# Decayed GLA keys turned on VectorE and placed through DRAM, where TensorE transposed them per pair

## The chip, the cores and the metric

The kernel runs on one core of one Trainium2 chip. The metric is the device time of one execution in microseconds (us), taken as the median of several runs. TensorE (PE) multiplies matrices and loads its weights (PEld), VectorE (DVE) and ScalarE (ACT) work elementwise on SBUF and PSUM, GpSimd (POOL) here mostly issues stores, and SyncE (SP) issues loads.

## What is computed

The reference is one layer of a hybrid trunk: a shared input projection, then gated linear attention (GLA), multi-scale pooling and cross-attention, gated, summed and projected. What the change touches is the GLA recurrence of the prompt (4 heads, 1024 tokens, key dimension 128, value dimension 256, blocks of 64 tokens):

```python
b = jnp.cumsum(ab, axis=3)
b_last = b[:, :, :, -1:]
q_dec = qb * jnp.exp(b)
k_inv = kb * jnp.exp(-b)
k_end = kb * jnp.exp(b_last - b)
att = jnp.where(mask, jnp.einsum('bhncd,bhnsd->bhncs', q_dec, k_inv), 0.0)
o_intra = jnp.einsum('bhncs,bhnse->bhnce', att, vb)
dS = jnp.einsum('bhncd,bhnce->bhnde', k_end, vb)
...
o_inter = jnp.einsum('bhncd,bhnde->bhnce', q_dec, S_before)
```

`k_end`, the decayed keys, is what is turned. It comes with the key dimension on the partitions and the tokens along the free axis. `dS` sums over tokens, so TensorE wants it with the tokens on the partitions.

## The kernel before

The prompt's GLA runs in 16 chunks: 4 heads with 4 chunks of 256 tokens, and each chunk in two pairs (even and odd) of 128 tokens. It fills the span from about 392 to 740 us, at some 21.6 us per chunk, and is interleaved on PE with the large products of the input projection (called px in the rows: groups of three matmuls, lines 242 to 244) and with the steps of the sample tokens and the cross-attention. PE and SP work in the order in which the program issues. DVE, ACT and POOL work in an order that a scheduler sets when the program is built.

For each chunk there are these functions:

- `gla_load` (L896) has SP load the log decays (alc) and the keys and queries (kq).
- `gla_gates` (L903) makes the decays (bz), and from them the decayed queries and both forms of the keys. The last row, L935, leaves k_end in kq.
- `gla_within` (L938), once per pair, computes the scores within a block in two matmuls of 64 columns each (L944, L945), transposes 128 columns of k_end on PE into the other half of the same PSUM tile (L946), masks the scores on DVE (L947), and splits the whole tile of 256 columns into a high part (ACT, L223) and a low part (DVE, L224), both in one tile called ak.
- `gla_recur` (L952), once per pair, multiplies by the values: `mm3` (L242 to L244) does a product from the high and low parts in three matmuls, once with the turned keys (into td) and once with the scores (into to). L963 adds the old state's part. Then the state is advanced (st, L968), and the output copied and squared on ACT (L976, L977).
- `gla_values`, `gla_split` load and split the values (v, vsh). `gla_out` turns the output in 32 x 32 blocks on DVE (L992) and stores it with four stores on POOL (L994).

`gla_steps` sets the order of these per chunk n: gates of n+1, split of n, the even pair's `gla_within`, the recurrence of the odd pair of chunk n-1, the odd pair's `gla_within`, the loads for later chunks, the recurrence of the even pair, and the output of chunk n-1. `R(...)` takes the next tile from a ring of 14 buffers that most of these steps share, so that a tile's first writer waits for the last reader of the tile that had that place before.

Of the kernel before, what the change touches and what calls it, by code (L numbers as in the profile page):

```python
# [9 lines left out]
F32 = mybir.dt.float32  # L10
F32R = mybir.dt.float32r
# [7 lines left out]
P = 128  # L19
# [5 lines left out]
NH = 4  # L25
# [22 lines left out]
def trunk_kernel(ctx: ExitStack, tc: tile.TileContext,  # L48
# [159 lines left out]
    al_scr = scratch(2, "als", (P, HT))  # L208
    q_scr, k_scr = (scratch(2, s, PAIR) for s in ("qsc", "ksc"))
    vt_scr = scratch(NH, "vtsc", (T, DV))  # L210
    u_scr, xq_raw = (scratch(4, s, PAIR) for s in ("usc", "xqsc"))
    mix_scr = [None if n == 0 else scratch(4, f"mixsc{n}_", (P, 2, T)) for n in range(3)]
    on_scr = scratch(NH, "onsc", (DV // 32, 32, 2, 4, 2, 64))
# [690 lines left out]
    def gla_gates(h, c):  # L904
# [29 lines left out]
        act(z, z, AF.Exp, scale=1.0 / TAU)  # L934
        nc.vector.tensor_tensor(k, k, z, op=ALU.mult)  # L935
        gla["g", h, c] = kq, kiqi, decp

    def gla_within(h, pr):  # L938

        c, cs = pr // 2, slice((pr % 2) * P, (pr % 2 + 1) * P)  # L940
        kq, kiqi, _ = gla["g", h, c]
        kt, qd, ki, qi = (x[:, cs] for x in (kq[:, 0], kq[:, 1], kiqi[:, 0], kiqi[:, 1]))
        t = PZ()
        nc.tensor.matmul(t[0:64, 0:P], lhsT=ki[:, 0:64], rhs=qi, start=True, stop=True)  # L944
        nc.tensor.matmul(t[64:P, 0:P], lhsT=ki[:, 64:P], rhs=qd, start=True, stop=True)  # L945
        nc.tensor.transpose(t[:, P:2 * P], kt, ident)  # L946
        nc.vector.copy_predicated(t[:, 0:P], nmask, zeros)  # L947
        ak = R([2, DV], F32R, name="ak")
        split(ak[:, 0], ak[:, 1], t[:, :DV])
        gla["w", h, pr] = ak[:, 0], ak[:, 1]  # L950

    def gla_recur(h, pr):  # L952
        c, cs = pr // 2, slice((pr % 2) * P, (pr % 2 + 1) * P)
        hi, lo = gla["w", h, pr]
        vh, vl = (x[:, pr % 2] for x in gla["vs", h, c])
        _, kiqi, decp = gla["g", h, c]
        st = gla.get(("st", h))
        t = PZ()
        td, to = t[:, :DV], t[:, DV:]
        mm3(td, hi[:, P:], lo[:, P:], vh, vl, True, True)  # L960
        mm3(to, hi[:, :P], lo[:, :P], vh, vl, True, st is None)
        if st is not None:
            nc.tensor.matmul(to, lhsT=kiqi[:, 1, cs], rhs=st, start=False, stop=True)  # L963
        s2 = wk.tile([P, DV], F32, tag="st", name="st", bufs=2)
        if st is None:
            nc.vector.tensor_copy(s2, td)
        else:
            nc.vector.scalar_tensor_tensor(s2, st, decp[:, pr % 2:pr % 2 + 1], td, op0=ALU.mult, op1=ALU.add)  # L968
        gla["st", h] = s2
        if pr == 7:  # L970
            nc.gpsimd.dma_start(out=o_gla_p[h], in_=s2)
        if pr % 2 == 0:
            sq = wk.tile([P, 2], F32, tag="sq", name="sq", bufs=3)
            gla["o", h, c] = R([2, DV], name="on"), sq
        on, sq = gla["o", h, c]
        nc.scalar.activation(on[:, pr % 2], to, AF.Copy)  # L976
        nc.scalar.activation(to, to, AF.Square, accum_out=sq[:, pr % 2:pr % 2 + 1])  # L977
        if pr % 2:
            r = rstd_of(sq, 1.0 / DV)
            for j in range(2):  # L980
                nc.scalar.activation(on[:, j], on[:, j], AF.Copy, scale=r[:, j:j + 1])
# [87 lines left out]
    def gla_steps():  # L1069
# [7 lines left out]
        for n in range(N + 1):  # L1077
# [5 lines left out]
            if n < N:  # L1083
                gla_split(h, c)
                gla_within(h, 2 * c)
                yield 2
            if n > 0:
                gla_recur(ph, 2 * pc + 1)
                yield 2
                yield next(samples, 0)  # L1090
            if n < N:
                gla_within(h, 2 * c + 1)
                yield 2
                yield next(samples, 0)
# [471 lines left out]
```

## Time and profile before

| | us |
|---|---|
| median of 3 runs | 1442.61 (1440.45 to 1442.92) |
| the profiled execution: its own time | 1445.01 |
| the profiled execution: its span | 1443.3 |
| PE busy | 1417.4 |
| DVE busy | 916.2 |
| ACT busy | 679.0 |
| POOL busy | 222.1 |

The page of the profile covers one execution. A row such as `396.34 0.75 DVE L224 ... x2` gives the start in us from the start of the span, the length, the engine, the line, the operation, out<-in with the tiles' names, the shape, and the count of instructions put together; a bracket at its end gives the idle time before it and what ended it. Rows of the chain of waits give start, length, engine, tile and line. The PE rows of the timeline overlap, since matmuls are pipelined; their steady distance is 0.12 us. The granted clock is 1.00 through the whole GLA stage.

### The profile page before, as it was taken

To read this page: it belongs to the slowest core of one execution; us is meant where nothing else is said; L and a number is where in the kernel's file an instruction comes from. 1 tells how busy PE (TensorE), PEld (TensorE's weight loads), DVE (VectorE), ACT (ScalarE), POOL (GpSimd) and SP (SyncE) were. 2 spreads that over 40 slices of the span, in tenths; PEclk is the share of its full clock that TensorE was granted. 3 is DMA by queue.
4 is the path that set the end of the run, shared out by engine and by line. 5 is a ranking of instruction groups with operands and counts; after the bars stand their busy time and mean duration, and the time that the engine had idled before them with its cause. 6 is when DMAs were issued, how large, how long until landed. Compare 5 with 4: busy or idle time off the path is not lost.

```text
span 1443.3 us, 28179 instructions
## 1 busy us (share of the span) xinstructions
PE 1417.4 (98%) x10689; PEld 1356.1 (94%) x10689; DVE 916.2 (63%) x2123; ACT 679.0 (47%) x1575; POOL 222.1 (15%) x401
## 2 busy tenths in 40 slices
PE   8999999999999999999999999999999999999998
PEld 6899999989899999999999999999999999999876
DVE  6954756666687777767766778785672434554436
ACT  6743544443465666656654445444472432233212
POOL 3211111124342121212221111111010000000000
PEclk9999999999999999999999999999999999999999
DMA  9355665656656363554654455454694777632633
GB/s 329 125 165 169 217 218 187 207 175 165 198 155 193 115 192 129 182 176 126 187 167 150 149 188 170 159 184 163 204 298 134 234 257 249 234 104 79 224 118 116
DMA packets 183507, 259.42 MB, mean 180 GB/s; under 512 B 22204, under 2 KB 132564, under 8 KB 183364
## 3 DMA queue, kind: packets, MB, share of 16 engines
q1 hardware_dynamic: 159900, 183.87, 41.5%
q0 software_dynamic: 23328, 73.56, 14.7%
q8 instruction: 84, 1.38, 0.4%
q14 instruction: 51, 0.42, 0.1%
q10 hardware_dynamic: 144, 0.20, 0.0%
HBM read 180.47 MB, written 77.56 MB: 179 GB/s over the span
## 4 chain that ended last, share of the span: by engine, by line
PE 88%; DMA 5%; DVE 5%; issue 1%; ACT 1%; SPq 0%; POOL 0%; DVEq 0%; ACTq 0%; POOLq 0%
PE px L242 25%; PE px L243 25%; PE px L244 25%; DMA qb<-xqs 3%; PE pz L244 2%; PE pz L243 2%; PE pz L242 2%; DMA raw<-in_w_in_dram 1%; DVE kc L777 1%; PE pz L963 1%; PE pz L404 1%; PE pz L944 1%; PE pz L817 1%; PE pz L946 1%; PE pz L907 0%
## 5 line engine op out<-in xcount | busy, mean ns | idle before, releaser
L244 PE MATMUL px<-bh,wbl 128*128 128x384 f32 (+1 forms) x576 | 184.1, 320 | 0.0
L243 PE MATMUL px<-bl,wbh 128*128 128x384 f32 (+1 forms) x576 | 184.1, 320 | 0.0
L242 PE MATMUL px<-bh,wbh 128*128 128x384 f32 (+1 forms) x576 | 183.7, 319 | 0.0
L554 ACT ACTIVATE r<-px 128x258 f32<-128x258 f32 x240 | 89.9, 375 | 47.4 <-PE px L244 46.9
L242 PEld LDWEIGHTS px<-bh,wbh 128*128 128x128 f32 x576 | 108.3, 188 | 0.0
L243 PEld LDWEIGHTS px<-bl,wbh 128*128 128x128 f32 x576 | 108.2, 188 | 0.0
L244 PEld LDWEIGHTS px<-bh,wbl 128*128 128x128 f32 x576 | 108.2, 188 | 0.0
L242 PE MATMUL px<-ot,s1h 128*128 128x258 f32 x320 | 94.1, 294 | 0.0
L242 PE MATMUL px<-o,a12h 128*128 128x258 f32 x320 | 93.4, 292 | 0.0
L242 PE MATMUL px<-ot,s3h 128*128 128x258 f32 x320 | 93.2, 291 | 0.0
L242 PE MATMUL px<-o,s4h 128*128 128x258 f32 x320 | 93.0, 291 | 0.2 <-DVE c L636 0.2
L242 PE MATMUL px<-o,a11h 128*128 128x258 f32 x320 | 92.8, 290 | 0.0
L242 PE MATMUL px<-ot,a22h 128*128 128x258 f32 x320 | 92.6, 289 | 0.0
L242 PE MATMUL px<-ot,s2h 128*128 128x258 f32 x320 | 92.2, 288 | 0.0
L243 PE MATMUL px<-o,a11h 128*128 128x258 f32 x320 | 91.1, 285 | 0.3 <-DVE o L224 0.3
L243 PE MATMUL px<-o,a12h 128*128 128x258 f32 x320 | 91.1, 285 | 0.0
L244 PE MATMUL px<-o,a12l 128*128 128x258 f32 x320 | 91.0, 284 | 0.0
L244 PE MATMUL px<-ot,s1l 128*128 128x258 f32 x320 | 90.9, 284 | 0.0
L243 PE MATMUL px<-ot,s1h 128*128 128x258 f32 x320 | 90.8, 284 | 0.0
L244 PE MATMUL px<-o,a11l 128*128 128x258 f32 x320 | 90.6, 283 | 0.0
L243 PE MATMUL px<-ot,s2h 128*128 128x258 f32 x320 | 90.1, 281 | 0.5 <-DVE ot L224 0.5
L243 PE MATMUL px<-ot,a22h 128*128 128x258 f32 x320 | 90.5, 283 | 0.0
(471 smaller groups left out, 4634.3 us busy)
## 6 DMA issues: line engine op xcount, KB each, us to landing
raw<-in_w_in_dram SPq DMA_DIRECT2D x80, 512.0 KB, 4.0
msc<-c POOLq DMA_DIRECT2D x24, 516.0 KB, 4.8
brsc<-c POOLq DMA_DIRECT2D x24, 516.0 KB, 3.7
sig<-msc SPq DMA_DIRECT2D x24, 516.0 KB, 6.0
brr<-brsc SPq DMA_DIRECT2D x48, 256.0 KB, 5.2
wbr<-in_w_branch_dram SPq DMA_DIRECT2D x24, 512.0 KB, 5.5
acc<-sig POOLq DMA_DIRECT2D x16, 516.0 KB, 5.2
acc<-acc SPq DMA_DIRECT2D x16, 516.0 KB, 7.0
```

Source lines behind the costliest of these rows:

```text
L242: nc.tensor.matmul(out, lhsT=lh, rhs=rh, start=start, stop=False, skip_group_check=more)
L243: nc.tensor.matmul(out, lhsT=lh, rhs=rl, start=False, stop=False, skip_group_check=more)
L244: nc.tensor.matmul(out, lhsT=ll, rhs=rh, start=False, stop=stop, skip_group_check=more)
L404: nc.tensor.matmul(t[:, :DV], lhsT=memT[k // 2][:, k % 2, a * P:(a + 1) * P], rhs=raw[k // 2][:, k % 2], start=k == 0, stop=k == NK - 1)
L554: nc.scalar.activation(r, acc[c][:, :QT], AF.Copy)
L777: nc.vector.tensor_tensor_reduce(kc[:, a, :], kc[:, a, :], qb[:, bb, :], scale=1.0, scalar=0.0, op0=ALU.mult, op1=ALU.add, accum_out=sc[:, ...
L817: nc.tensor.matmul(t[32 * j:32 * j + 32, :DV], lhsT=pm[:, a, 4 * i + j, :], rhs=vc[j][:, a, :], start=a == 0, stop=a == 1)
L944: nc.tensor.matmul(t[0:64, 0:P], lhsT=ki[:, 0:64], rhs=qi, start=True, stop=True)
L946: nc.tensor.transpose(t[:, P:2 * P], kt, ident)
L963: nc.tensor.matmul(to, lhsT=kiqi[:, 1, cs], rhs=st, start=False, stop=True)
```

## The change

The transpose on PE goes. `gla_gates` now turns the whole k_end of a chunk on DVE in 32 x 32 blocks (kt) and has POOL store it in four pieces, each of 32 partitions, to a scratch in DRAM (ktsc), so that the blocks land where a full transpose would have them. A new function, `gla_turned`, has SP load the turned keys of a chunk (ktr), and another, `gla_keys`, splits them once per chunk for both pairs: ACT writes the high part, DVE the low part in place. The tile ak now holds only the scores of both pairs, 128 columns each. Per chunk, the ring gives out ten tiles where it gave nine.

```diff
--- before.py
+++ after.py
@@ -208,6 +208,7 @@
     al_scr = scratch(2, "als", (P, HT))
     q_scr, k_scr = (scratch(2, s, PAIR) for s in ("qsc", "ksc"))
     vt_scr = scratch(NH, "vtsc", (T, DV))
+    kt_scr = scratch(4 * NH, "ktsc", (CT, P))
     u_scr, xq_raw = (scratch(4, s, PAIR) for s in ("usc", "xqsc"))
     mix_scr = [None if n == 0 else scratch(4, f"mixsc{n}_", (P, 2, T)) for n in range(3)]
     on_scr = scratch(NH, "onsc", (DV // 32, 32, 2, 4, 2, 64))
@@ -934,31 +935,45 @@
         act(z, z, AF.Exp, scale=1.0 / TAU)
         nc.vector.tensor_tensor(k, k, z, op=ALU.mult)
         gla["g", h, c] = kq, kiqi, decp
+        kt = R([CT], name="kt")
+        nc.vector.transpose(kt, k)
+        for q in range(4):
+            nc.gpsimd.dma_start(out=kt_scr[4 * h + c][:, 32 * q:32 * q + 32].rearrange("(b r) k -> r b k", r=32),
+                                in_=kt[32 * q:32 * q + 32].rearrange("r (b k) -> r b k", k=32))
+
+    def gla_turned(h, c):
+        t = gla["kt", h, c] = R([2, 2, P], F32R, name="ktr")
+        nc.sync.dma_start(out=t[:, 0].bitcast(F32), in_=kt_scr[4 * h + c].rearrange("(j p) k -> p j k", j=2))
+
+    def gla_keys(h, c):
+        t = gla["kt", h, c]
+        split(t[:, 1], t[:, 0], t[:, 0].bitcast(F32))
 
     def gla_within(h, pr):
 
         c, cs = pr // 2, slice((pr % 2) * P, (pr % 2 + 1) * P)
         kq, kiqi, _ = gla["g", h, c]
-        kt, qd, ki, qi = (x[:, cs] for x in (kq[:, 0], kq[:, 1], kiqi[:, 0], kiqi[:, 1]))
+        qd, ki, qi = (x[:, cs] for x in (kq[:, 1], kiqi[:, 0], kiqi[:, 1]))
         t = PZ()
         nc.tensor.matmul(t[0:64, 0:P], lhsT=ki[:, 0:64], rhs=qi, start=True, stop=True)
         nc.tensor.matmul(t[64:P, 0:P], lhsT=ki[:, 64:P], rhs=qd, start=True, stop=True)
-        nc.tensor.transpose(t[:, P:2 * P], kt, ident)
         nc.vector.copy_predicated(t[:, 0:P], nmask, zeros)
-        ak = R([2, DV], F32R, name="ak")
-        split(ak[:, 0], ak[:, 1], t[:, :DV])
-        gla["w", h, pr] = ak[:, 0], ak[:, 1]
+        if pr % 2 == 0:
+            gla["ak", h, c] = R([2, 2, P], F32R, name="ak")
+        ak = gla["ak", h, c][:, pr % 2]
+        split(ak[:, 0], ak[:, 1], t[:, :P])
 
     def gla_recur(h, pr):
         c, cs = pr // 2, slice((pr % 2) * P, (pr % 2 + 1) * P)
-        hi, lo = gla["w", h, pr]
+        hi, lo = (gla["ak", h, c][:, pr % 2, i] for i in range(2))
+        kl, kh = (gla["kt", h, c][:, i, pr % 2] for i in range(2))
         vh, vl = (x[:, pr % 2] for x in gla["vs", h, c])
         _, kiqi, decp = gla["g", h, c]
         st = gla.get(("st", h))
         t = PZ()
         td, to = t[:, :DV], t[:, DV:]
-        mm3(td, hi[:, P:], lo[:, P:], vh, vl, True, True)
-        mm3(to, hi[:, :P], lo[:, :P], vh, vl, True, st is None)
+        mm3(td, kh, kl, vh, vl, True, True)
+        mm3(to, hi, lo, vh, vl, True, st is None)
         if st is not None:
             nc.tensor.matmul(to, lhsT=kiqi[:, 1, cs], rhs=st, start=False, stop=True)
         s2 = wk.tile([P, DV], F32, tag="st", name="st", bufs=2)
@@ -1084,11 +1099,13 @@
                 gla_split(h, c)
                 gla_within(h, 2 * c)
                 yield 2
+                gla_turned(h, c)
             if n > 0:
                 gla_recur(ph, 2 * pc + 1)
                 yield 2
                 yield next(samples, 0)
             if n < N:
+                gla_keys(h, c)
                 gla_within(h, 2 * c + 1)
                 yield 2
                 yield next(samples, 0)
```

Over the whole program PE has 32 rows fewer and otherwise the same order. SP has 16 loads more, POOL 64 stores more. On DVE and ACT, rows have changed places beside those that are new. Three places follow. Line numbers of the changed program are one higher than before up to L935, and 11 to 15 higher behind it. In the names, c is a product of the input projection, r a copy of another, ws and raw are the weights and sums of them with their split parts (a11h, s4l and so on), vt the values turned for their store.

On DVE, at the first chunk, the rows of before from the second transpose of vt to the sums of weights:

```order
L587 STREAM_TRANSPOSE vt<-c_4995 128x512
L619 TENSOR_TENSOR c_5101<-px,r_4947 128x258
L935 TENSOR_TENSOR kq<-kq,bz 128x256
L224 TENSOR_TENSOR a11l<-raw,a11h 128x512
L224 TENSOR_TENSOR v<-v,vsh 128x512
L947 COPY_PREDICATED pz<-nmask,zeros 128x128 x2
L224 TENSOR_TENSOR s4l<-ws,s4h 128x512
L224 TENSOR_TENSOR ak<-pz,ak 128x256 x2
L305 TENSOR_TENSOR ws<-raw 128x512
L305 TENSOR_TENSOR ws<-ws,raw 128x512
```

And the same place now:

```order
L306 TENSOR_TENSOR ws<-raw 128x512
L933 TENSOR_TENSOR bz<-blp,bz 128x256
L960 COPY_PREDICATED pz<-nmask,zeros 128x128
L225 TENSOR_TENSOR s4l<-ws,s4h 128x512
L936 TENSOR_TENSOR kq<-kq,bz 128x256
L306 TENSOR_TENSOR ws<-ws,raw 128x512
L939 STREAM_TRANSPOSE kt<-kq 128x256
L588 STREAM_TRANSPOSE vt<-c_5017 128x512 x2
L225 TENSOR_TENSOR v<-v,vsh 128x512
L225 TENSOR_TENSOR ak<-pz,ak 128x128 x2
L225 TENSOR_TENSOR ktr<-ktr 128x256
```

Both sums ws, the new transpose kt and the two transposes vt now stand ahead of ak.

On DVE, around the gates that are worked out during chunk 2 (those of chunk 3), before (s are states of the sample tokens):

```order
L224 TENSOR_TENSOR a11l<-raw,a11h 128x512
L619 TENSOR_TENSOR c_5845<-px,r_5703 128x258
L619 TENSOR_TENSOR c_5845<-px,r_5717 128x258
L1031 SCALAR_TENSOR_TENSOR s_5957<-vb,smp,s_5957 128x256 x2
L224 TENSOR_TENSOR s4l<-ws,s4h 128x512
L305 TENSOR_TENSOR ws<-ws,raw 128x512
L891 TENSOR_SCALAR bz<-pz,vec 128x256
L1031 SCALAR_TENSOR_TENSOR s_5961<-vb,smp,s_5961 128x256 x2
L894 TENSOR_TENSOR bz<-bz 128x256
L911 SCALAR_TENSOR_TENSOR bz<-smask,bz 128x256
```

And now, from the same gates on:

```order
L892 TENSOR_SCALAR bz<-pz,vec 128x256
L225 TENSOR_TENSOR a22l<-raw,a22h 128x512
L895 TENSOR_TENSOR bz<-bz 128x256
L1046 SCALAR_TENSOR_TENSOR s_6004<-vb,smp,s_6004 128x256
L912 SCALAR_TENSOR_TENSOR bz<-smask,bz 128x256
L1046 SCALAR_TENSOR_TENSOR s_6004<-vb,smp,s_6004 128x256
L918 TENSOR_TENSOR decp<-dec 128x2
L921 COPY blp<-bz 128x2
L922 TENSOR_TENSOR blp<-bz 128x2
L927 TENSOR_TENSOR kq<-kq,bz 128x256
L620 TENSOR_TENSOR c_5888<-px,r_5745 128x258
L620 TENSOR_TENSOR c_5888<-px,r_5759 128x258
```

The two rows of c have gone from ahead of the gates to behind their row of kq.

On ACT, at chunk 11, before (on is the output, rr the root of its norm):

```order
L223 ACTIVATE vsh<-v 128x512
L223 ACTIVATE ak<-pz 128x256
L655 ACTIVATE c_8703<-px 128x258
L223 ACTIVATE s3h<-ws 128x512
L75 ACTIVATE bz<-bz 128x256
L976 ACTIVATE on<-pz 128x256
L977 ACTIVATE pz,sq<-pz 128x256
L75 ACTIVATE rr<-rv 128x2
L75 ACTIVATE rr<-rr 128x2
L223 ACTIVATE a11h<-raw 128x512
L223 ACTIVATE ak<-pz 128x256
L981 ACTIVATE on<-on,rr 128x256 x2
```

And now:

```order
L224 ACTIVATE s3h<-ws 128x512
L75 ACTIVATE bz<-bz 128x256
L224 ACTIVATE vsh<-v 128x512
L224 ACTIVATE ak<-pz 128x128
L991 ACTIVATE on<-pz 128x256
L992 ACTIVATE pz,sq<-pz 128x256
L224 ACTIVATE a11h<-raw 128x512
L75 ACTIVATE rr<-rv 128x2
L75 ACTIVATE rr<-rr 128x2
L224 ACTIVATE ak<-pz 128x128
L224 ACTIVATE ktr<-ktr 128x256
```

The first ak of each piece is that of the even pair, the second that of the odd pair; the split of the turned keys stands behind the second.

## The prediction

> **What bounds the kernel now.** First the head of the page, then its chain of work that ended last.
>
> ```profile
> span 1443.3 us, 28179 instructions
> PE 1417.4 (98%) x10689; PEld 1356.1 (94%) x10689; DVE 916.2 (63%) x2123; ACT 679.0 (47%) x1575; POOL 222.1 (15%) x401
> PE 88%; DMA 5%; DVE 5%; issue 1%; ACT 1%; SPq 0%; POOL 0%; DVEq 0%; ACTq 0%; POOLq 0%
> ```
>
> TensorE (PE) is busy for 98% of the span and makes up 88% of the chain. The change touches only the GLA stage, so the windows of that stage come next (busy time and count of PE, weight loads, DVE, ACT, POOL, then granted clock, DMA share and GB/s).
>
> ```profile
> 395.00:480.00 85.00, 84.34 (x687) 80.84 (x686) 66.81 (x169) 51.37 (x142) 29.79 (x50) 1.00 0.56 158
> 480.00:560.00 80.00, 80.00 (x657) 76.22 (x656) 59.02 (x157) 49.86 (x142) 17.66 (x31) 1.00 0.55 171
> 560.00:640.00 80.00, 80.00 (x656) 76.18 (x655) 58.96 (x158) 49.72 (x138) 14.88 (x24) 1.00 0.48 157
> 640.00:745.00 105.00, 105.00 (x863) 99.90 (x862) 76.25 (x201) 62.87 (x180) 21.95 (x36) 1.00 0.54 162
> ```
>
> From 395 to 745 us, PE stands still for 85.00 - 84.34 = 0.66 us in all, at the full clock. Two things follow. What is taken from PE here comes off the time, since nothing else is late. And PE runs a fixed order, so each microsecond by which DVE, ACT or a load is newly late at a place where PE needs it goes onto the time. DVE is busy for 261 of these 350 us and ACT for 214: they have room on the average, but each works through a queue, and what counts is where in it a row stands.
>
> **What the removed transposes are worth.** One transpose of the decayed keys goes per pair, 32 in all. Its price is read from the chain: start, length, instruction; first around the removed row, then where another group of column-tiled matmuls (L1048, 32 columns wide) runs straight into a full-width product.
>
> ```profile
> 414.69 0.12 PE px L244
> 414.81 0.25 PE pz L944
> ...
> 415.18 0.26 PE pz L946
> 415.44 0.13 PE px L242
> ...
> 445.05 0.57 PE pz L1048 x8
> 445.62 0.32 PE px L242
> 445.94 0.12 PE px L243
> ...
> 480.79 0.57 PE pz L1048 x8
> 481.36 0.32 PE px L242
> 481.68 0.12 PE px L243
> ```
>
> The transpose L946 takes 0.26 us of the chain, so 32 of them are 32 x 0.26 = 8.3 us at most. But L944 and L945 ahead of it are column-tiled as well (64 columns), and the rows of L1048 show that the first full-width matmul behind such a group takes 0.32 us where its like takes 0.12. So about 0.20 us belongs to leaving the tiled group, not to the transpose, and it will fall on the next L242 when L946 is gone. Before: 0.26 + 0.13 = 0.39 us. After: 0.32 us. Saved: 0.07 us a pair, 32 x 0.07 = **2.2 us**. The ends are 0 and 8.3 us; I take 2.2, since the nearest rows show the very transition that remains. [...]
>
> **What is added beside PE.** Rows of the GLA stage (line, operation, count, busy time, mean ns, idle before), then two DMA rows (KB each, us to landing):
>
> ```profile
> L992 DVE STREAM_TRANSPOSE go<-on 128x512 f32<-128x512 f32 x16 | 11.3, 705 | 0.0
> L224 DVE TENSOR_TENSOR ak<-pz,ak 128x256 fp32r<-128x256 f32 x32 | 13.4, 421 | 3.5 <-ACT ak L223 3.5
> L929 DVE TENSOR_TENSOR kiqi<-kq,dec 128x128 f32<-128x128 f32 x14 | 4.0, 285 | 0.0
> L223 ACT ACTIVATE ak<-pz 128x256 fp32r<-128x256 f32 x32 | 11.9, 377 | 7.3 <-DVE pz L947 6.2 <-DVE kq L935 0.7
> L994 POOL DMA_DIRECT2D onsc<-go x64 | 37.4, 590 | 51.6 <-DVE go L992 43.7 <-DVE rv L253 4.5 <-DVE ws L305 2.9
> onsc<-go POOLq DMA_DIRECT2D x64, 64.0 KB, 2.5
> kq<-ksc SPq DMA_DIRECT2D x16, 128.0 KB, 3.9
> ```
>
> The DVE transpose kt is half of L992's size: between 0.35 and 0.71 us, I take 0.35. DVE gets 16 x (0.35 + 0.42) = 12.3 us and loses 32 x (0.421 - 0.285) = 4.4 us on the halved ak: about +8 us on 261. ACT gets 16 x 0.38 = 6 us and loses some 4. POOL gets 64 x 0.59 = 38 us on 84. None of the three is full, so the work itself costs PE nothing; the cover is the free fourth of DVE. If it were gone, the 8 us would go onto the time.
>
> The four stores have as many runs as L994's, of half the length (128 bytes), and should land in about 2.5 us, 3.1 at most taking the other rows of stores on that queue as a guide. They are issued a whole chunk (about 21.6 us) ahead of the load that reads them. [...]
>
> The load of the turned keys can go when its slot in the ring is free, and the last reader of that slot is the recurrence of the odd pair before. For chunk 11:
>
> ```profile
> 638.79 0.43 PE pz L963 x2
> ...
> 645.62 0.12 PE pz L242
> ```
>
> Free at 639.2, landed 3.9 us later at 643.1, split by ACT (0.38) and DVE (0.42) at 643.9; the recurrence that reads it starts on PE at 645.62. That is **1.7 us to spare**, and the other chunks look alike. So the load by itself is in time, provided that SP issues it at once and that ACT and DVE are free for the split.
>
> **Where the new order makes PE late.** PE's order stays as it was but for the transposes. DVE's and ACT's rows are placed anew (the three places are shown with the change), and I compared, for each value that PE needs, when it is needed in the trace of before with when its engine reaches it in the new order. Four places fall behind.
>
> *Chunk 0, DVE.*
>
> ```profile
> 391.94 0.71 DVE L587 STREAM_TRANSPOSE vt<-c 128x512 f32<-128x512 f32 x1
> ...
> 396.34 0.75 DVE L224 TENSOR_TENSOR ak<-pz,ak 128x256 fp32r<-128x256 f32 x2
> 397.00 0.69 DVE L305 TENSOR_TENSOR ws<-raw 128x512 f32<-128x512 f32 x1
> 397.72 0.69 DVE L305 TENSOR_TENSOR ws<-ws,raw 128x512 f32<-128x512 f32 x1
> ...
> 396.90 0.38 PE L1001 MATMUL pz<-ident,smp 128*8 128x128 f32 x2 [0.66 <-DVE ak L224]
> ```
>
> PE already waits 0.66 us there for ak. DVE is back to back before it. In the new order, the second ws, the new kt transpose and both vt transposes stand ahead of ak. The vt are only moved, but ws (0.6) and kt (0.35) come on top, and the row that used to be ended by 396.8 is reached at 398.6: **+1.8 us**. Nothing behind it gives this back, since PE has no idle time.
>
> *Chunk 2, ACT.* The split of the turned keys stands behind the ak of the odd pair, which needs the mask of the pair's matmuls; in the trace that ak begins at 438.99 and the recurrence is on PE at 439.63:
>
> ```profile
> 438.99 0.37 ACT L223 ACTIVATE ak<-pz 128x256 fp32r<-128x256 f32 x1
> 439.63 0.12 PE pz L242
> ```
>
> ACT's half then ends at 439.36 + 0.38 = 439.7 and DVE's half, behind its own ak, at 440.5: **+0.8 us**.
>
> *Chunk 3, DVE.* The two rows c<-px that free the PSUM of a product slide behind the chain of the gates:
>
> ```profile
> 444.00 0.75 DVE L619 TENSOR_TENSOR c<-px,r 128x258 f32<-128x258 f32 x2
> 452.91 0.42 DVE L926 TENSOR_TENSOR kq<-kq,bz 128x256 f32<-128x256 f32 x1
> 451.86 0.28 PE L242 MATMUL px<-o,a11h 128*128 128x258 f32 x1
> ```
>
> They ran at 444.0. Behind L926 they are reached at 453.3, while PE wants the freed buffer at 451.86: **+1.5 us**. Part of the gates' chain (the sample rows of L1031 ahead of it) hangs on loads that don't move with PE.
>
> *Chunk 11, ACT.* As in chunk 2, with a wider gap:
>
> ```profile
> 646.30 0.38 ACT L223 ACTIVATE ak<-pz 128x256 fp32r<-128x256 f32 x1 [1.88 <-DVE pz L947]
> 646.85 0.42 DVE L224 TENSOR_TENSOR ak<-pz,ak 128x256 fp32r<-128x256 f32 x1
> ```
>
> The odd pair's ak could be late before, as it was not needed until a chunk half later. Now the keys for PE's 645.62 queue behind it: ACT at 647.1, DVE at 647.7, **+2.0 us**.
>
> **The sum.** 1.8 + 0.8 + 1.5 + 2.0 = 6.1 us of new waits, less 2.2 us: **+3.9 us**. The profiled execution took 1445.0 us by itself, so its like would take 1448.9. The median of the runs is 1442.6, and the forecast is set against that: **1446.5 us**. Each wait is between 0 (a value that comes earlier since ak is half as long) and about twice what I give it (a wait that makes the next place late too).
>
> **The rivals.**
>
> *All of it hidden* (0.25). The halved ak rows (0.14 us less each on DVE) and PE's own lateness pull the places together: once PE is 1.8 us late from chunk 0, rows that hang on loads have that much longer, so waits need not add up. For it: places 2 and 3 are smaller than the first. Against it: in chunks 2 and 11 the late row itself hangs on PE, and slides with it. Time: 1442.6 - 2.2 = 1440.4 us.
>
> *The transposes are worth their whole 0.26 us* (0.15). This is the rival on the other side. If the 0.20 us at the edge belongs to what the tiled groups of 32 columns leave behind, not to those of 64, the next L242 takes 0.12. Against it: L944 itself takes 0.25 at its start, an edge of the same size. Then 8.3 us go, and with between none and 4 us of the waits the time is 1434 to 1438, about 1436 us. It decides from 0.20 us a pair on, where the gain (6.4 us) passes the waits.
>
> *The load is late in each chunk* (0.15). SP issues in its own order, and stands long in front of full buffers:
>
> ```profile
> 400.02 13.00 SPq L296 DMA_DIRECT2D raw<-in_w_in_dram  x2
> ```
>
> Queued behind such a row is the load of the turned keys, and behind that in ACT's queue stand the copies out of PSUM. With 1.7 us to spare, any delay beyond that goes to PE. One microsecond in each of chunks 1 to 15, with chunk 0's 1.8 and the 2.2 saved: +14.6, or about 1457 us. Against it: SP gets to the load ahead of the slot's release in most chunks by the trace of before.
>
> *The forecast* (0.45), from 1442 to 1450 us by itself.
>
> **How the numbers follow.** A run of this kernel can be told from no change beyond 0.2%, 2.9 us: faster is below 1439.7, slower above 1445.5. The forecast lies four fifths on the slow side (0.35) and one fifth within (0.10); the hidden case is within (0.20) or a bit faster (0.05); the third case is faster (0.15), the last slower (0.15). So faster 0.20, within 0.30, slower 0.50. The range goes from 1437 (a large gain, with some of the waits) to 1453 (the sum of the waits doubled: 12.2 - 2.2 = +10); outside lie most of the late loads and the bottom of the full gain, some 0.2.
>
> **What would show it.** On the chain of after, the L242 behind L945 at 0.32 us bears out the 2.2, at 0.12 the 8.3. The windows from 395 to 745 should show some 6 us of PE idle instead of 0.66: about 2 us before L1001 put down to ak, about 1 and 2 us before the recurrences of chunks 2 and 11 put down to ktr, 1.5 before a product put down to c or kq. PE idle of about a microsecond ahead of every recurrence would show the late load; no idle at all, with a shorter stage, would show that the order of rows did not matter and that I was wrong in counting waits from the old times.

## The result, and the profile after

The changed kernel takes **1456.3 us** (median of 4 runs, 1454.9 to 1460.2) where the kernel before takes 1441.9 beside it (4 runs): the ratio is 1.010, with a 95% interval of 1.0084 to 1.0115. It is slower by about 14.4 us, above the range of the prediction. The profiled execution took 1460.2 us by itself, 15.2 more than that of before, and is the one all rows of after are from.

The head of the page of after:

```profile
span 1458.4 us, 28357 instructions
PE 1419.7 (97%) x10657; PEld 1356.4 (93%) x10657; DVE 921.9 (63%) x2155; ACT 679.5 (47%) x1591; POOL 258.2 (18%) x465
```

PE has 32 rows fewer and is still busy for 2.3 us more, and the span has grown by 15.1 us. No engine has become full on the average: DVE has 6 us more, POOL 36. So most of the loss is in waiting. The windows of the GLA stage of after (columns as in the prediction) say where:

```profile
395.00:480.00 85.00, 74.49 (x582) 70.19 (x582) 59.22 (x155) 44.97 (x129) 38.67 (x67) 0.96 0.59 166
480.00:560.00 80.00, 80.00 (x654) 76.16 (x653) 59.64 (x161) 47.98 (x140) 22.80 (x41) 1.00 0.54 171
560.00:640.00 80.00, 78.11 (x623) 74.82 (x623) 61.08 (x166) 49.34 (x141) 22.82 (x38) 0.98 0.52 156
640.00:745.00 105.00, 103.86 (x849) 98.36 (x848) 75.74 (x204) 63.13 (x180) 31.60 (x52) 1.00 0.57 170
```

Before, PE stood still for 0.66 us in the first window; now it does for 85.00 - 74.49 = 10.5 us there, and 3.0 in the last two. Two windows also have a granted clock below 1. The waits of PE in the stage (engine, tile, line, what it waited for: us in total, times, longest), after:

```profile
PE px L243 <- DVE c L620: 5.9, 1, 5.9
PE pz L1016 <- DVE ak L225: 3.3, 1, 3.3
PE pz L958 <- DVE ak L225: 1.9, 1, 1.9
PE pz L958 <- ACT pz L992: 1.1, 1, 1.1
PE pz L1078 <- ACT os L1072: 0.8, 1, 0.8
PE pz L243 <- ACT ktr L224: 0.7, 1, 0.7
```

Each is a single wait, at one chunk. Since PE's order is the same in both kernels, its rows can be paired one by one, and the start of each in after less its start in before tells how late PE is at that point:

```
start before  start after  late   place
   395.97       395.07    -0.90   ahead of chunk 0
   397.48       399.19    +1.71   behind the wait for ak at L1016 (chunk 0)
   439.10       441.59    +2.49
   439.95       443.64    +3.69   behind the wait for ktr (chunk 2)
   451.63       455.34    +3.71
   451.98       462.04   +10.06   behind the wait for c (chunk 3)
   454.89       466.35   +11.45   matmuls at half the clock
   550.43       561.30   +10.87
   550.92       563.76   +12.84   behind the wait for ak at L958 (chunk 7)
   554.91       569.17   +14.26   matmuls at half the clock
   641.73       655.47   +13.74
   642.22       657.17   +14.95   behind the wait for L992 (chunk 11)
   747.80       762.14   +14.34
   748.35       763.61   +15.26   last sample step
   999.88      1015.12   +15.24
```

The whole 15.2 us arise between 396 and 748 us; with the 0.90 us by which this execution came early to the stage, the stage costs 16.2. (The profiled executions of the runs below with 14 tiles in the ring come to it between 0.2 and 4.0 us early, so what a stage costs is read from the lateness at its end less that at its start.) Between the jumps the lateness sinks slowly (11.45 to 10.87, 14.26 to 13.74): that is the gain of the transposes.

### The profile page after: what moved, and what is told of

The parts are those of the page before. It is cut to its first block, busy times and chain, and to the rows that moved or that the text cites. A ratio compares the mean times of both kernels' runs of the same rounds, so it can differ in the third digit from the quotient of the medians.

```text
span 1458.4 us, 28357 instructions
## 1 busy us (share of the span) xinstructions
PE 1419.7 (97%) x10657; PEld 1356.4 (93%) x10657; DVE 921.9 (63%) x2155; ACT 679.5 (47%) x1591; POOL 258.2 (18%) x465
## 3 DMA queue, kind: packets, MB, share of 16 engines
q0 software_dynamic: 25376, 75.66, 15.2%
## 4 chain that ended last, share of the span: by engine, by line
PE 79%; DMA 8%; DVE 8%; ACT 2%; issue 2%; SPq 0%; POOL 0%; DVEq 0%; ACTq 0%; POOLq 0%
PE px L243 23%; PE px L244 23%; PE px L245 23%; DMA qb<-xqs 3%; PE pz L245 2%; PE pz L244 2%; PE pz L243 2%; DMA vb<-vs 2%; DMA raw<-in_w_in_dram 2%; DVE kc L778 1%; PE pz L405 1%; DVE ws L306 1%; PE pz L818 1%; DMA s<-in_state_gla_dram 1%; PE pz L958 1%
## 5 line engine op out<-in xcount | busy, mean ns | idle before, releaser
L243 PE MATMUL px<-bh,wbh 128*128 128x384 f32 (+1 forms) x576 | 183.7, 319 | 0.0
L243 PEld LDWEIGHTS px<-bh,wbh 128*128 128x128 f32 x576 | 108.4, 188 | 0.0
L243 PE MATMUL px<-o,a11h 128*128 128x258 f32 x320 | 94.1, 294 | 5.9 <-DVE c L620 5.9
L243 PE MATMUL px<-ot,s1h 128*128 128x258 f32 x320 | 94.1, 294 | 0.0
L243 PE MATMUL px<-ot,s3h 128*128 128x258 f32 x320 | 93.7, 293 | 0.0
L243 PE MATMUL px<-o,a12h 128*128 128x258 f32 x320 | 93.5, 292 | 0.0
L243 PE MATMUL px<-o,s4h 128*128 128x258 f32 x320 | 93.0, 291 | 0.1
L243 PE MATMUL px<-ot,a22h 128*128 128x258 f32 x320 | 92.7, 290 | 0.0
L243 PE MATMUL px<-ot,s2h 128*128 128x258 f32 x320 | 92.2, 288 | 0.0
L245 PE MATMUL px<-ot,s3l 128*128 128x258 f32 x320 | 90.8, 284 | 0.0
L244 PE MATMUL px<-ot,s3h 128*128 128x258 f32 x320 | 90.7, 283 | 0.0
```

The costliest lines, as they stand in the source:

```text
L243: nc.tensor.matmul(out, lhsT=lh, rhs=rh, start=start, stop=False, skip_group_check=more)
L244: nc.tensor.matmul(out, lhsT=lh, rhs=rl, start=False, stop=False, skip_group_check=more)
L245: nc.tensor.matmul(out, lhsT=ll, rhs=rh, start=False, stop=stop, skip_group_check=more)
```

## The experiments

The theory of the prediction is that the new work costs PE nothing and that what costs is old rows of DVE and ACT that stand later (A in the expectations). Against it stands that the added work itself holds up the queues and the memory (B). Beside them there were two ideas of why the rows moved: the tenth tile per chunk out of the full ring (R in the expectations), or the scheduler's own estimates, which any new row shifts (S). Many runs set rows to a place by hand. They all use this addition, with a list of row numbers for each engine:

```diff
+    place_rows(nc, tc, nosync)
+def place_rows(nc, tc, nosync):
+    for engine, packed in ROWS.items():
+        traced = [i for i in nc.cur_bb.bb.instructions if str(i.engine) == "EngineType." + engine]
+        row = json.loads(zlib.decompress(base64.b85decode(packed)))
+        for a, b in zip(row, row[1:]):
+            tc.add_manual_dep(traced[b], traced[a].name, nosync, reason="row")
```

It only sets an order within an engine; it adds no wait between engines.

**new_order_alone**: the kernel before, its old rows in the order they have in after.

```diff
 # before, and place_rows with
+ROWS = {"DVE": <order of after without kt, ktr>, "Activation": <the same>, "Pool": <the same>}
```

> The kernel before, with all of its work and its transposes on PE, but with its rows on DVE, ACT and POOL placed in the order that the changed kernel has (its new rows left out). Theory A (the time comes from the places of the old rows in the queues, not from the added work): nearly the whole loss is there, 10 to 15 us above before, that is 1452 to 1457 us, with a wait of about 5 to 6 us for the rows c of chunk 3 and 2 to 3 us for ak at chunk 0. Theory B (the added stores, loads and splits hold up the queues and the memory): none of that work is here, so within 3 us of before.

Measured: 1454.4 us, ratio 1.0072 (1.0054 to 1.0089), about +10.4. Its largest waits:

```profile
PE pz L1001 <- DVE ak L224: 3.0, 1, 3.0
PE px L242 <- DVE c L619: 2.5, 1, 2.5
PE pz L944 <- ACT pz L977: 2.0, 1, 2.0
```

So a loss of most of that size comes with no new instruction at all: it is the order of rows that were there before. But it is not the same loss. The wait for c is 2.5 us where 5 to 6 were expected and after has 5.9, and by the paired rows chunk 11 costs 3.6 us here (with a stretch at half the clock; the mean clock is 0.995, that of before 0.997) and 1.2 in after. What makes the wait for c as long as in after is not the order alone.

**old_order**: all of the change, but the old rows in the order of before, the new ones fitted in.

```diff
-        kt = R([CT], name="kt")
-        nc.vector.transpose(kt, k)
+        nc.vector.transpose(z, k)
 # and place_rows with
+ROWS = {"DVE": <order of before, with kt and ktr>, ...}
```

> The changed kernel with all of its new work, but every old row on DVE, ACT and POOL in the order of before, and the new rows put into gaps of that order; the turned keys are written over the tile z, which is free by then, so that the ring of 14 gives out nine tiles per chunk as before. Theory A: the waits of the changed kernel at chunks 0, 3, 6 and 11 are gone, and what is left is the 2.2 us that PE saves, less at most 1 us at chunk 0 where the first turned keys are only just in time: 1440 to 1441 us, 1 to 2 us below before. Theory B: the work is the same as in the changed kernel, so 8 to 14 us above before.

Measured: 1448.6 us, ratio 1.0032 (1.0019 to 1.0045). It gains 7.7 us on after and misses the level that was expected. Its waits of PE have one new row, and DVE's timeline, idle time in brackets, shows what is ahead of it:

```profile
PE pz L1026 <- DVE ak L225: 3.7, 1, 3.7
```

```profile
407.58 0.23 DVE L929 COPY kiqi<-kq 128x128 f32<-128x128 f32 x1 [4.02 <-PE pz L245]
```

DVE stands in its queue for 4.02 us until a recurrence has read the tile whose place in the ring kiqi takes. The order of before fitted tiles that came free sooner; with ak and ktr kept for both pairs it no longer fits. So the new tiles do seem to cost something here, and not as work; that is read from this row, and no run tested it. Behind this wait too the clock was halved (0.50 from 413.14 to 419.97 us).

**no_transpose**: the kernel before without L946, its rows in the order of before. The recurrence takes the scores where it took the turned keys, so the result is not that of the layer, and the splits are half as wide.

```diff
-        nc.tensor.transpose(t[:, P:2 * P], kt, ident)
...
-        ak = R([2, DV], F32R, name="ak")
-        split(ak[:, 0], ak[:, 1], t[:, :DV])
+        ak = R([2, DV], F32R, name="ak")[:, :, :P]
+        split(ak[:, 0], ak[:, 1], t[:, :P])
```

> The kernel before without the 32 transposes of the decayed keys on PE and with nothing in their place: the scores stand in for the turned keys in the recurrence, and the splits have 128 columns. All rows of DVE, ACT and POOL stay in the order of before, so this is the PE saving by itself. If leaving a column-tiled group costs 0.20 us whatever follows: 32 x 0.07 = 2.2 us less, about 1440 us, and the first L242 behind L945 takes 0.32 us of the chain. If the transpose is worth its whole 0.26 us: 8.3 us less, about 1434 us, and that L242 takes 0.12.

Measured: 1440.25 us (12 runs) against 1441.86, ratio 0.9983 (0.9971 to 0.9995): 1.6 us by the medians, 2.4 by the ratio (0.7 to 4.2). The forecast of 2.2 holds and 8.3 is out. The chain of this run shows why:

```profile
411.73 0.10 PE pz L944
411.84 0.32 PE px L242
```

The product behind the scores now pays the 0.32 us itself.

**c_ahead**: the changed kernel, with two rows of DVE moved back to where they were.

```diff
 a11l<-raw,a11h            (DVE, near 442 us)
+c<-px,r  x2
 ...
 kq<-kq,bz                 (gates, near 461 us)
-c<-px,r  x2
```

> The changed kernel with two rows of DVE in another place: the two rows c<-px of chunk 3 are put ahead of the sample states and the gates again, directly behind a11l, where they stood before; all else stays in the order of the changed kernel. Theory A: the longest wait (5.9 us) and the slow matmuls behind it (about 1 us) go, so 6 to 7 us below the changed kernel, about 1449 to 1450 us. If the chain of loads and not the place in the queue is what PE waits for: the wait turns up at the next row behind the gates, and the time stays at 1455 to 1457 us.

Measured: 1449.4 us, ratio 1.0052 (1.0034 to 1.0069): 6.9 us less than after. Its largest waits:

```profile
PE pz L1016 <- DVE ak L225: 3.3, 1, 3.3
PE pz L958 <- DVE ak L225: 1.4, 2, 1.1
```

The wait of 5.9 us and the slow matmuls behind it are gone, and nothing of them comes back. In this order, half of the loss hangs on the place of two rows.

**c_behind**: the kernel before, with only these two rows moved behind the gates' kq.

```diff
-c<-px,r  x2               (DVE, 444.0 us)
 ...
 kq<-kq,bz                 (gates, 452.9 us)
+c<-px,r  x2
```

> The kernel before with one thing changed: the two rows c of chunk 3 on DVE stand behind the gates' row kq. That is the one term of the prediction that was put at 1.5 us. If its size comes from the place alone: a wait of 1.5 to 2 us at the next product, time 1 to 3 us above before. If the place alone makes a wait as long as in the changed kernel: 5 to 7 us above before.

Measured: 1447.6 us, ratio 1.0028 (1.0014 to 1.0041), about +4, between the two forecasts. Its largest wait of PE, and then windows of PE with the granted clock in the third column from the right:

```profile
PE px L242 <- DVE c L619: 2.7, 1, 2.7
```

```profile
455.00:457.00 2.00, 2.00 (x12) 1.50 (x11) 2.00 (x6) 0.81 (x2) 0.99 (x1) 0.50 0.45 158
457.00:459.00 2.00, 2.00 (x14) 2.00 (x14) 0.51 (x2) 0.73 (x3) 0.78 (x2) 0.70 0.35 134
```

The prediction's term for this place was 1.5. The place alone costs a wait of 2.7 us, and then 2.00 x 0.50 + 2.00 x 0.30 = 1.6 us more, since the clock is halved behind the wait. In after the same place costs 5.9 and 1.4, so something else made it worse there.

**usc_ahead**: the changed kernel, with the store usc (and the copy ahead of it) put ahead of the four new stores in POOL's row.

```diff
+smp<-c, usc<-c            (POOL, near 440 us)
 ktsc<-kt  x4
-smp<-c, usc<-c
```

> The changed kernel with two rows of POOL in another place: the copy and the store usc of chunk 3's product go ahead of the four stores of kt, behind which they had waited (442.4 us in the changed kernel, 430.5 before). If the stores crowded together at 440 to 445 us are what makes the load vb land late (8.5 us against 5.1 before) and so lengthen the 5.9 us wait: vb lands in 5 to 6 us, the wait falls to 2.5 to 4 us, and the time by 2 to 4 us, to 1452 to 1454 us. If not, the wait and the time stay as in the changed kernel.

Measured: 1455.55 us, ratio 1.0082 (1.006 to 1.0104).

```profile
PE px L243 <- DVE c L620: 3.9, 1, 3.9
```

The wait for c falls from 5.9 to 3.9 us as expected, so the place of that store does move the wait. The load vb lands in 6.5 us where 5 to 6 were expected. The time falls by 0.8 us by the medians and by 2.6 by the ratios, whose intervals overlap, so the 2 to 4 us forecast are neither shown nor ruled out. In the profiled execution the stage cost 1.7 us less than in after. By the paired rows the slow matmuls behind the wait for c cost 2.1 us where they cost 1.4 in after; those behind chunk 7, where PE waits 1.7 us here, are gone, and some have come behind the wait of chunk 0, where after has none.

**kt_in_z**: the changed kernel with nine tiles per chunk from the ring (kt goes over z, which is free by then), rows as the scheduler then sets them.

```diff
-        kt = R([CT], name="kt")
-        nc.vector.transpose(kt, k)
+        nc.vector.transpose(z, k)
```

> The changed kernel with one edit: kt is written over the tile z, which nothing reads any more by then, so that the ring gives out nine tiles per chunk as before and not ten; rows stand where the scheduler puts them. Theory R: some of the pressure is gone, 3 to 8 us above before (the turned keys still hold their tile longer than ak did). Theory S: another set of places with waits of its own, which may lie anywhere from 0 to 15 us above before.

Measured: 1453.8 us, ratio 1.0079 (1.0062 to 1.0096). With the ring as full as before, the wait for c is there again, at 7.8 us. The tenth tile is not what places c behind the gates: R is not borne out. (c is then placed behind other rows as well: it runs at 458.18 us, and kq ran at 453.96.)

**ring16** and **before_ring16**: 16 tiles in the ring, and one less in the other large pool to make room, in the changed kernel and in the kernel before.

```diff
-NE = 30
-NR = 14
+NE = 29
+NR = 16
```

> The changed kernel with 16 tiles in the ring where it has 14, and one tile fewer (29) in the large pool of operands to make room. Theory R (the changed kernel keeps more tiles of the ring in use, and this is why its rows were moved and why engines wait for a tile): with room in the ring the long waits go, and it comes out 1 to 3 us below its control, the kernel before with the same two pools. Theory S (the places of the rows came out unluckily, whatever the ring): waits of 8 us or more in the GLA stage stay, and it lies 8 to 15 us above its control.

> The control: the kernel before with the same two pools (16 tiles in the ring, 29 in the large pool). If the pools matter little to it, within 3 us of before, 1439 to 1445 us; if one operand tile fewer holds it up, above that, and then only its difference to the run with the change counts.

Measured: 1513.9 (ratio 1.0481, 1.0449 to 1.0512) and 1489.4 us (1.0305, 1.0283 to 1.0328). The changed kernel lies 24.5 us above its control, which is against R (1 to 3 us below) and beyond S (8 to 15 above). But the two sizes together cost the kernel before some 45 us already, so little can be read from the pair.

**before_ring13**: the kernel before with one tile less.

```diff
-NR = 14
+NR = 13
```

> The kernel before with 13 tiles in the ring where it has 14, no other edit, rows where the scheduler puts them. Theory R (one tile more in use is enough to move rows and to make engines wait): 4 to 12 us above before, with waits in the GLA stage for ak or c. If a tile fewer does nothing: within 3 us of before.

Measured: 1458.2 us, ratio 1.0108 (1.008 to 1.0135). By PE's paired rows almost all of it arises ahead of 380 us, in other stages, and some 2 us in the GLA stage. The ring is short, but this does not tell what places the rows.

**mended**: kt_in_z with the late rows moved up.

```diff
 # DVE: c x2 back behind a11l (chunk 3); ak and st ahead of weight rows (chunk 7)
 # ACT: ak, on, sq ahead of s4h (chunk 7);  POOL: smp, usc ahead of the four stores (chunk 3)
+ROWS = {...}
```

> The run kt_in_z with seven rows in other places and nothing else: on DVE the two rows c of chunk 3 directly behind a11l again, and at chunk 7 st and ak ahead of the next split; on ACT at chunk 7 ak and the two rows of the output ahead of s4h; on POOL the copy and the store usc of chunk 3 ahead of the four stores of kt. Theory A with D (PE waits where a row that it needs stands behind one that need not be there; all the rest of the added work is covered): the waits of 7.8 and 1.3 us and the slow matmuls behind them go, 9 to 11 us below kt_in_z, 1443 to 1445 us, level with before or up to 2 us above. If the added work costs by itself, other waits take their place and it stays 5 us or more above before.

Measured: 1445.5 us (12 runs), ratio 1.002 (1.0008 to 1.0032): 8.3 less than kt_in_z, where 9 to 11 were forecast. The largest waits left:

```profile
PE px L243 <- DVE c L637: 2.4, 1, 2.4
PE pz L1015 <- DVE ak L225: 1.3, 1, 1.3
```

**mended2**: mended, with the two c of L637 moved up too, and the row r of ACT that one of them needs.

```diff
 kq<-kq,bz                 (DVE, L927)
+c<-px,r (L637)
 s<-vb,smp,s
+c<-px,r (L637)
 ...
-c<-px,r (L637)  x2
```

> As in mended, with the two rows c<-px of the last level of chunk 3 (L637) and the ACT row r of the second of them moved up as well, to about 454 us, ahead of the gates' rows kiqi. Theory (only the places of rows cost time; the new work itself costs PE nothing): the wait of PE for c of 2.4 us at 457.69 falls to under 0.5 us and the half clock behind it (1.2 us) goes: 1445.5 - 3 = 1442 to 1443 us, ratio 1.000 (0.999 to 1.001), thus level with the kernel before, since what is left (about 1.3 us before the recurrence of chunk 0, 0.6 of ktr, 0.3) about equals the transposes' 2.2. Rival (there is a cost of the new work beside the waits, such as the stores or the loads, that moves to the next place): the wait turns up elsewhere and the time stays at 1444.5 to 1446 us, ratio 1.0015 to 1.0025.

Measured: 1444.95 us (12 runs), ratio 1.0013 (1.0001 to 1.0024). The largest waits of PE, and windows behind the place:

```profile
PE pz L1015 <- DVE ak L225: 1.3, 1, 1.3
PE pz L957 <- DVE ak L225: 1.2, 1, 1.2
```

```profile
456.00:458.00 2.00, 2.00 (x18) 1.95 (x17) 2.00 (x8) 1.15 (x3) 0.00 (x0) 1.00 0.92 256
458.00:460.00 2.00, 2.00 (x19) 1.95 (x17) 1.97 (x6) 1.66 (x5) 0.01 (x1) 1.00 0.67 191
460.00:462.00 2.00, 0.82 (x8) 0.50 (x7) 2.00 (x5) 0.84 (x5) 2.00 (x4) 1.00 0.80 241
```

The wait for c is gone, and the half clock behind it, but 3 us later a wait of 1.2 us for ak has come. The median lies in the rival's range and the ratio between the two (the theory's goes up to 1.001, the rival's begins at 1.0015), so the time does not decide. That a wait came up elsewhere is the rival's sign. The windows show why: DVE (third pair) is busy for 2.00 + 1.97 + 2.00 = 5.97 of 6 us around that ak. Whether there is too much work in this stretch, or only a bad order once more, is open: on DVE the splits s2l (0.68 us) and v (0.69 us) stand right ahead of ak, PE first reads s2l at 468.93 us, and no run put ak ahead of them.

## Why the prediction went wrong, step by step

**What bounds the kernel.** Right. PE's busy time is nearly the same, its order too, and each wait in the stage went onto the time: the lateness never sinks again but for the transposes.

**The transposes (2.2 us).** Right. The chain of after, at a pair far from any wait, shows the edge as forecast:

```profile
604.05 0.10 PE pz L958
...
604.16 0.32 PE px L243
```

0.26 + 0.13 has become 0.32 us, and no_transpose measured 1.6 to 2.4 us. The edge of 0.32 us stayed and moved to the next matmul (L243 here, L242 at 411.84 us in no_transpose).

**The added work.** Right for the loads and stores, by the DMA rows of after (KB each, us to landing; from 400 to 470 us):

```profile
vb<-vs SPq DMA_DIRECT2D x4, 256.0 KB, 8.5
ktsc<-kt POOLq DMA_DIRECT2D x12, 32.0 KB, 2.2
ktr<-ktsc SPq DMA_DIRECT2D x3, 128.0 KB, 2.3
```

The stores land in 2.2 us (2.5 taken), the load in 2.3 (3.9 taken). So the third rival, the load that is late in each chunk, which gave 1457 us, comes near the time and is wrong in its mechanism: PE waited for ktr once, for 0.7 us. The DVE transpose took 0.44 us, within its bounds (0.35 taken). "None of the three is full, so the work itself costs PE nothing" holds on the average only. In the stretch of mended2 DVE was full, and the best order that was tried left about 1.9 us (ratio 1.0013), where the forecast without waits was 2.2 us of gain. And the first row of the list above, vb, is what the step left out: what the new transfers may do to the old ones.

**The four waits (6.1 us).** This is the step that failed: in the size of one term above all (chunk 3), in a place that it left out (chunk 7), and in the half clock behind both, which it put at nothing.

- *Chunk 0, +1.8.* The place, the engine and the reason were right, the size too small. PE waits 3.3 us where it waited 0.66, so 2.6 more. That L1016 starts at 398.62, the very time of the forecast, is luck: PE came 0.9 us early here, and in c_ahead and usc_ahead, where it came 2.4 and 4.0 us early, it waited the same 3.3. The wait moves with PE. Nor do the terms of the forecast, 0.6 + 0.35, make 1.8: both sums of weights went ahead of ak, and 0.69 + 0.69 + 0.35 come near it.
- *Chunk 2, +0.8.* Right in kind: ktr from ACT, and PE is 1.2 us later behind it.
- *Chunk 11, +2.0.* Wrong. PE waited 1.1 us for L992 at L958 ahead of the recurrence, and ktr was in time behind that.
- *Chunk 3, +1.5.* The row and the engine were right, and the size wrong: 6.35 us, and 1.4 at the slow clock. The step took the gates' kq at its time of before. This term alone is 6.2 us (6.35 + 1.4 - 1.5) of the 9.8 by which the median missed the forecast.
- *Chunk 7* was not in the list: 2.0 us for ak at L958, and 1.4 at the slow clock. The comparison of the new order with the old times did not find it. With st and ak moved up there the wait is gone (1.3 us in kt_in_z, none left in mended), so it too is a matter of place.

**How chunk 3 came to 5.9 us.** The prediction put c behind the gates' kq and took kq at its time of before, 453.3. But kq itself came at 460.85. SP's and ACT's timelines before:

```profile
440.04 0.63 SPq L1024 DMA_DIRECT2D vb<-vs  x1
446.31 0.37 SPq L670 DMA_DIRECT2D s<-in_state_gla_dram  x1
...
447.74 0.47 ACT L890 ACTIVATE bz<-pz,vec 128x256 f32<-128x256 f32 x1 [0.53 <-PE pz L907]
```

SP, ACT and DVE after:

```profile
443.58 0.51 SPq L1039 DMA_DIRECT2D vb<-vs  x1
453.12 0.37 SPq L671 DMA_DIRECT2D s<-in_state_gla_dram  x1
...
456.02 0.51 ACT L1045 ACTIVATE s<-s,as 128x256 f32<-128x256 f32 x1 [3.26 <-DMA s<-in_state_gla_dram]
456.44 0.46 ACT L891 ACTIVATE bz<-pz,vec 128x256 f32<-128x256 f32 x1
...
452.21 0.88 DVE L1046 SCALAR_TENSOR_TENSOR s<-vb,smp,s 128x256 f32<-128x256 f32 x2 [4.67 <-ACT r L555]
456.93 0.48 DVE L892 TENSOR_SCALAR bz<-pz,vec 128x256 f32<-128x256 f32 x1 [2.50 <-ACT bz L891]
460.85 0.43 DVE L927 TENSOR_TENSOR kq<-kq,bz 128x256 f32<-128x256 f32 x1
461.19 0.76 DVE L620 TENSOR_TENSOR c<-px,r 128x258 f32<-128x258 f32 x2
```

And what SP waited for ahead of that s:

```profile
SPq L671 <- DMA vb<-vs: 8.0, 1, 8.0
SPq L671 <- DVE s L1046: 1.0, 1, 1.0
```

Read from the top: the load vb is issued 3.5 us later (443.58 against 440.04). That adds nothing to the wait, since PE itself is 2.5 to 3.7 us late there; the prediction had held that these loads don't move with PE. But vb then takes 8.5 us where its like took 5.1. DVE's sample row can thus start at 452.1, and it does at 452.21. (The profile names ACT's r there, which had long been done; in c_ahead the same row is put down to vb.) Only behind it does SP issue the next state s, 6.8 us later than before. ACT stands 3.26 us in front of that s, and in ACT's queue the gates' first row is behind it: 456.44 against 447.74. From there DVE goes through the gates and reaches c. So a product of the input projection waits for the gates, these for a sample token's state, and this for a load that landed late.

The four runs with the two rows right behind the gates' kq bear this out. Where vb lands in 5.0 us (new_order_alone), 5.7 (c_behind), 6.5 (usc_ahead) and 8.5 (after), PE waits for c for 2.5, 2.7, 3.9 and 5.9 us: the place alone makes about 2.5, and the late landing the rest.

Why vb lands late is less clear. Its median landing from 400 to 470 us:

```
before 5.1   new_order_alone 5.0   no_transpose 5.2   c_behind 5.7      (no turned keys)
after 8.5    c_ahead 7.9   mended2 7.3   kt_in_z 7.2   usc_ahead 6.5   mended 6.4   old_order 5.7
```

Where the four stores and the load are absent, vb lands in 5.0 to 5.7 us; where they are there, in 5.7 to 8.5: in 5.7 to 7.3 with usc ahead of the four stores (old_order, mended, usc_ahead, mended2) and in 7.2 to 8.5 with it behind them. POOL's row in after is full from 439.94 to 444.5 with these stores and those of the samples. That they delay vb fits these eleven runs; it was not isolated, since no run kept the order of after and left only the stores out.

**The slow clock** was not in the sum at all. In the traces of before and after the granted clock falls to 0.50 for 3.41 us, once, in after, for 6.83 (the last stretch, at the end of the span, aside), and in each of them all these stretches start whole multiples of 3.41 us apart: at 124.50 and 366.85 us before, at 124.12, 366.47, 458.63 and 564.44 us in after. So the stage of after is cut here at these places: first around the wait of chunk 0, then around those of chunk 3 and chunk 7:

```profile
393.78:397.19 3.41, 1.57 (x12) 1.37 (x12) 3.41 (x9) 1.66 (x6) 0.38 (x1) 1.00 0.73 193
397.19:400.60 3.41, 1.98 (x17) 1.99 (x18) 1.91 (x5) 0.93 (x3) 3.41 (x7) 1.00 0.48 95
400.60:404.01 3.41, 3.41 (x29) 3.35 (x28) 1.82 (x4) 2.21 (x7) 3.41 (x6) 1.00 0.69 97
...
455.22:458.63 3.41, 0.51 (x5) 0.31 (x3) 0.97 (x2) 2.61 (x7) 0.00 (x0) 1.00 0.32 86
...
462.04:465.46 3.42, 3.42 (x17) 2.86 (x17) 2.26 (x8) 0.74 (x3) 0.00 (x0) 0.50 0.01 3
...
561.03:564.44 3.41, 1.52 (x14) 1.14 (x13) 3.31 (x10) 2.44 (x9) 1.77 (x4) 1.00 0.06 10
564.44:567.85 3.41, 3.41 (x19) 3.41 (x18) 2.55 (x10) 2.39 (x7) 0.57 (x1) 0.50 0.73 180
```

And usc_ahead, cut at its own places, around the same wait of chunk 0:

```profile
392.09:395.51 3.42, 0.19 (x2) 0.00 (x0) 3.42 (x9) 0.61 (x3) 1.77 (x4) 1.00 0.77 205
395.51:398.92 3.41, 3.37 (x16) 3.32 (x17) 0.52 (x2) 1.06 (x3) 3.41 (x6) 0.50 0.51 76
```

The wait of 3.3 us at chunk 0 is split by an edge in after: PE stands still for 3.41 - 1.57 = 1.84 us in one window and 1.43 in the next, and the clock stays. In usc_ahead it falls into one window (3.42 - 0.19 = 3.23 us still), and the next is at half the clock. At chunk 7 it takes 3.41 - 1.52 = 1.89 us. The half clock costs 1.4 + 1.4 us in after. PE is "busy" in the windows at 462.04 and 564.44 us (3.42 of 3.42 and 3.41 of 3.41 us), so only the granted clock, 0.50, shows it.

**The sum.** By the paired rows the jumps at the four places are 2.6 + 1.2 + 6.4 + 1.2 = 11.4 (6.1 forecast), chunk 7 adds 2.0, the slow clock 2.8, smaller steps 2.0, and the transposes take off 2.0: 16.2 us from 396 to 748. The assumption that a wait could be at most twice its term failed because each term was worked out with all other rows at their times of before.

**How much is order, how much is the new work.** The order alone costs 10.4 us (new_order_alone). If the parts add up, that leaves about 14.4 - 10.4 + 2.2 = 6 us to the new work in that order, with each of the two times known to some 2 us. With nine rows put back it is 1445.5, with three more 1444.95 us. No kernel with the turned keys beat the kernel before. **Open** is why the scheduler placed c behind the gates: neither the tenth tile (kt_in_z) nor a shorter ring (before_ring13) shows it, and its own estimates were not tried.

## What to carry to other kernels

In a stage where one engine is full and the others follow in fixed queues, a change that adds small work is priced by what its rows push back, not by their duration: follow each late row to what stands ahead of it in its queue, and that on to the loads, until the chain reaches something that truly did not move. Two old rows moved by the scheduler made half of the loss here; try first to put such rows back by hand, before the idea is given up. And the waits of TensorE had a price beyond their length here: where one filled 1.89 us or more of a 3.41 us window in the GLA stage of after, the clock was halved behind it and the slow matmuls cost 1.4 us more, so a forecast of such waits needs a term for it.

## What the runs showed of the hardware

- **Half a clock, window by window.** In before and in after all stretches at half the clock start on a grid of 3.41 us, that at the end of the span too (1442.05 and 1455.32 us). It does not lie at one place in all runs: in usc_ahead an edge is at 395.51 us, in after at 397.19. Cut at this grid, from 12 us on, where the records of the clock begin, three windows at full clock in before and five in after were followed by one at half; PE stood still in them for 1.68 us or more (1.68 ahead of 124.50 us in before and of 124.12 in after, 1.89 ahead of 564.44, 2.4 to 3.4 in the others). Every full-clock window there with 1.89 us or more was followed so, none below 1.68, and from 1.68 to 1.84 both came (1.81 ahead of 1438.63 us in before and 1.84 ahead of 397.19 in after went free). So what counted here was not the length of a wait but how much of it fell into one window: the 3.3 us of chunk 0 went free in after (1.84 and 1.43 us) and not in usc_ahead (3.23, then 0.50 from 395.51 us), and 1.9 us in after, 2.4 in mended (then 0.53 from 459 to 461 us) and 2.7 in c_behind (then 0.50 from 455 to 457 us) did not. The slow clock behind a wait cost 1.4 us in after, twice, by the paired rows, and 1.6 in c_behind by its windows.
- **The edge of a column-tiled group** cost 0.20 us here (0.32 us for the L242 behind L1048 in before, whose like takes 0.12), and it moved to the next full-width matmul when the transpose was gone (0.32 us for L243 in after and for L242 in no_transpose). So the step removed from behind such a group saved less than it showed: 0.07 of 0.26 us.
- **A load landed later beside small stores.** In after the 32 KB stores landed in 2.2 us, yet the 256 KB loads vb beside them took 8.5 us by the median, where they took 5.1 in before. That the stores are the cause was not isolated.
